# Five pairs in blocks in the mixer's three middle projections, with a pair's block sums in a tile of their own

## Chip, cores and metric

The kernel runs on one core of a Trainium2 chip. The metric is device time in microseconds, the median of several runs; a profiled execution gives the trace. The core has a matrix engine (PE; its weight loads stand on a row of their own, PEld), a vector engine (DVE), a scalar engine (ACT), GpSimd (POOL, here mostly an issuer of DMAs that add to their target) and SP (an issuer of plain DMAs).

## What is computed

One layer of a decoder trunk on x of 256 rows x 2048 columns, float32: a feed-forward half step, a mixer of two head groups (differential attention and an mLSTM) between one combined input and one output projection, a second feed-forward half step and a last norm.

```python
x = x + 0.5 * swiglu(rmsnorm(x, ffn1_norm[l]), ffn1_w_gate[l], ffn1_w_up[l], ffn1_w_down[l])
h = rmsnorm(x, mix_norm[l])
a_q, a_k, a_v, m_q, m_k, m_v, m_o, m_i, m_f = jnp.split(h @ w_in[l], split_idx, axis=-1)
...
x = x + jnp.concatenate([y_a, y_b], axis=-1) @ w_out[l]
x = x + 0.5 * swiglu(rmsnorm(x, ffn2_norm[l]), ffn2_w_gate[l], ffn2_w_up[l], ffn2_w_down[l])
return rmsnorm(x, final_norm)
```

Nearly all of the work is x (256 rows) times a weight matrix.

## The kernel before

**Products.** Weights and x are float32. Each is split in two parts of a shorter format, high and low (`split`, L130 to L133: ACT casts the high part, DVE subtracts it to get the low part), and a product is three matmuls: high x high (L181), low x high (L182) and high x low (L184), each with a stationary 128x128 piece of x and a moving 128x512 piece of the weights.

**Plain units and pairs in blocks.** Two column chunks of weights, `wa` and `wb`, of 512 columns each are worked together (`Paired`). The 2048 rows of the weights are 16 k tiles, or 8 pairs of k tiles. A pair in plain products takes, for each of the two chunks, 2 k tiles x 2 halves of x's rows: 8 products. A pair in blocks is treated as a 2x2 block matrix times a 2x2 block matrix, with seven products instead of eight (Strassen's scheme in Winograd's form): A1, A2 and B2 with pieces of x and S1, S2, S3, S4 with sums of pieces of x (`sums`, L344 to L350). The weights need sums as well, which are made in place in a `raw` tile of three pieces: two at once by DVE (L480), a second by DVE (L498) or by a DMA of POOL that adds (L496), a third by such a DMA from a later load (`late`, L534). `ns` is the number of pairs in blocks; the rest is plain. L496 is used where `ns` is over 3, for all but the last two (or the last lone) of the pairs; `twos` groups the pairs by two.

**Stages of one `Paired`.** `leading` makes A1 and S1 for each two pairs; `sums` S2, A2 (`bare`, into the accumulator `accn`) and S3; `second` B2 and S4, mixed with plain units of the first chunk; `third` is the plain units of the second chunk. `Chain.run` interleaves `third` of one `Paired` with `leading` of the next. Small work of the mixer (convolutions, gates, scores, transposes) is put in lists (`side`, `mid`, `pending`), one entry of which is taken at each step of these stages.

**x's pieces.** In `sum_pair` a pair of x gets two tiles of the pool `slots` (22 tiles of 4 KB a partition), `hi` and `lo`, of eight 128x128 pieces each: four of x itself and four sums. A pair that is only used in plain products has one tile with both (`plain_pair`). In the mixer x's pairs are made by `chunk_to_xt` while the first feed-forward part ends; the first `NP_MIX` of eight pairs have sums.

**Where blocks are used.** In the feed-forward parts `ns` is 5 for the gate and up projections. In the mixer come one q/k `Paired` of narrower chunks (392 and 384 columns, 2 pairs in blocks), and then five of two 512-column chunks of `w_in`, with `NPS_MIX` pairs in blocks; the three middle ones are at about 771 to 970 us.

**Order.** A scheduler orders each engine's instructions by priority, by the order in which the program names them and by the tiles that are free; DMAs wait in their issuer's queue in that order. `rsq` (L291 to L296) computes a power on POOL, so that it stands in POOL's queue among DMA issues.

Of the kernel before, what the change touches and what calls it, by code (L numbers as in the profile page):

```python
# [10 lines left out]
F32R = mybir.dt.float32r  # L11
# [6 lines left out]
P = 128  # L18
D = 2048
S = 256  # L20
# [11 lines left out]
NEG = -1.0e30  # L32
UK = 2
NP = 5
NP_MIX = 4
NPS_MIX = (3,4,4,4,3)
NP_QK = 2
NP_OUT = 3
NP_FIRST = 3
# [16 lines left out]
G_FFN1, G_MIX, G_FFN2, G_CW, G_CB, G_ATT, G_ML = 0, 16, 32, 48, 80, 88, 96  # L56
# [4 lines left out]
def tile_trunk_layer(ctx: ExitStack, tc: tile.TileContext, x, xt, par, bias_if, lamv, fnorm,  # L61
# [4 lines left out]
    slots = ctx.enter_context(tc.tile_pool(name="slots", bufs=22))  # L66
# [11 lines left out]
    def nm(s):  # L78
        uid[0] += 1
        return f"{s}_{uid[0]}"  # L80


    prm = const.tile([P, N_PAR], F32, name="prm")
# [41 lines left out]
    def split_gain(src, gcol, hi, lo):  # L125

        nc.scalar.activation(hi, src, AF.Copy, scale=prm[:, gcol:gcol + 1])
        nc.vector.scalar_tensor_tensor(lo, src, prm[:, gcol:gcol + 1], hi.bitcast(F32),
                                       op0=ALU.mult, op1=ALU.subtract)

    def split(src, hi, lo):
        return (nc.scalar.copy(hi, src),  # L132
                nc.vector.tensor_tensor(out=lo, in0=src, in1=hi.bitcast(F32), op=ALU.subtract))  # L133
# [11 lines left out]
    def ahead_of_splits(i, ins, slack=SLACK):  # L145
        queued[i].append((len(splits) + slack, ins))
# [38 lines left out]

    def halves(xp, k, hb):

        hi, lo = xp[k // 2]
        i = 2 * (k % 2) + hb
        return hi[:, i, :], lo[:, i, :]  # L190

    def plain_pair(xp, j):

        t = slots.tile([P, 2, UK, S], F32R, tag="s", name=nm("xt"))
        xp[j] = tuple(t[:, i, :, :].rearrange("p a (b c) -> p (a b) c", b=NT) for i in range(2))
        return t[:, 0, :, :], t[:, 1, :, :]

# [27 lines left out]
    def in_turn(load):  # L225
        for early in turns[-1:]:
            after(load, early)
        turns.append(load)
# [13 lines left out]
    def units(accs, xp, w, nk, last_units=1, ahead=None, w0=0, banks=None):  # L242
# [9 lines left out]
        def products(hbs, u, rh, rl):  # L252
            ks = [(t, u * UK + t) for t in range(UK)]
            mms([(accs[hb], *halves(xp, k, hb), rh[:, t, :], rl[:, t, :], k == 0 and not (one and hb),
                  k == nk - 1, one) for hb in hbs for t, k in ks])
# [51 lines left out]
    def chunk_to_xt(c, gbase, xp, ns, now=KD):  # L307


        def run(j):  # L310
            tr = ps_tr.tile([P, 2, S], F32, tag="tr", name=nm("tr"))
            for i in range(2):
                for hb in range(NT):
                    nc.tensor.transpose(tr[:, i, hb * P:(hb + 1) * P],  # L314
                                        xres[:, hb, (2 * j + i) * P:(2 * j + i + 1) * P], ident)
            with tc.high_priority(offset=AHEAD):
                if j < ns:
                    sum_pair(xp, j, gained(tr, prm[:, gbase + 2 * j:gbase + 2 * j + 2]), j >= now)
                else:
                    hi, lo = plain_pair(xp, j)  # L320
                    for i in range(2):
                        split_gain(tr[:, i, :], gbase + 2 * j + i, hi[:, i, :], lo[:, i, :])

        pending.extend(functools.partial(run, j) for j in (2 * c, 2 * c + 1))
# [4 lines left out]
    def gained(src, gain):  # L329
        g = wk("xg")  # L330
        for i in range(2):
            ahead_of_splits(0, act.activation(g[:, i * S:(i + 1) * S], src[:, i, :], AF.Copy, scale=gain[:, i:i + 1]))
        return g.rearrange("p (a b) -> p a b", b=P)

    def sum_tiles(xp, j):
        xp[j] = tuple(slots.tile([P, 8, P], F32R, tag="s", name=nm("xs")) for _ in range(2))
        return xp[j]

    def sum_pair(xp, j, g, put_off=False):
        hi, lo = sum_tiles(xp, j)  # L340
        split(g, hi[:, 0:4, :], lo[:, 0:4, :])
        (side.append if put_off else lambda f: f())(functools.partial(sums, g, hi, lo))

    def sums(g, hi, lo):  # L344
        s = wk("xsum").rearrange("p (a b) -> p a b", b=P)
        tt = nc.vector.tensor_tensor
        tt(out=s[:, 0:2, :], in0=g[:, 0:2, :], in1=g[:, 1:4:2, :], op=ALU.subtract)
        tt(out=s[:, 2, :], in0=s[:, 1, :], in1=g[:, 0, :], op=ALU.subtract)
        tt(out=s[:, 3, :], in0=g[:, 2, :], in1=s[:, 2, :], op=ALU.add)
        split(s, hi[:, 4:8, :], lo[:, 4:8, :])  # L350

    def add_part(acc, hb, c):

# [9 lines left out]
    def residual(accs, c, scale, parts):  # L363
        for hb in range(NT):
            add_half(accs[hb], xres[:, hb, c * CW:(c + 1) * CW], scale)
        for hb in range(NT):
            square_sum(xres[:, hb, c * CW:(c + 1) * CW], parts[:, hb, c:c + 1])
# [19 lines left out]
    def wk(name):  # L387
        return work.tile([P, CW], F32, tag="w", name=nm(name))
# [28 lines left out]
    side, mid = [], []  # L417
# [6 lines left out]
    class Paired:  # L424
# [10 lines left out]
            self.raws = []  # L435

        def job(self, acc, j, xi, w, wi, first, last, on=False):
            xh, xl = self.xp[j]
            return acc, xh[:, xi, :], xl[:, xi, :], w[0][:, wi, :], w[1][:, wi, :], first, last, on

        def load(self, j):
# [253 lines left out]


    xp1 = {}
    gs = []

    xraws = {}  # L700

    def load_xt(u, t=None):
        k, i = u * UK, u % 2 * UK
        with tc.high_priority(offset=AHEAD):
            if i == 0 and not t:
                xraws[u // 2] = slots.tile([P, 2 * UK, S], F32, tag="s", name=nm("xraw"))
            both = xraws[u // 2]
            raw = both[:, i:i + UK, :]
            if t is not None:
                in_turn(nc.sync.dma_start(raw[:, t, :], xt[:, k + t, :]))  # L710
            elif u < 2:
                in_turn(nc.sync.dma_start(raw, xt[:, k:k + UK, :]))
            elif i == 0:
                nc.sync.dma_start(both, xt[:, k:k + 2 * UK, :])
            if u < NP:
                if not t:
                    gs.append((raw, u, *sum_tiles(xp1, u)))
                hi, lo = gs[-1][2:]
                hi, lo = (t[:, 0:4, :].rearrange("p (a b) c -> p a (b c)", a=2) for t in (hi, lo))
            else:  # L720
                hi, lo = plain_pair(xp1, u)
            for j in range(UK) if t is None else (t,):
                split_gain(raw[:, j, :], G_FFN1 + k + j, hi[:, j, :], lo[:, j, :])
        if u >= KD // UK - FIRST_IN:
            sum_xt()
        if u >= KD // UK - NT:

            hb = u - (KD // UK - NT)
            with tc.high_priority(offset=AHEAD - XLATE):
                nc.sync.dma_start(xres[:, hb, :], x[hb * P:(hb + 1) * P, :])  # L730

    def sum_xt():

        raw, j, hi, lo = gs.pop(0)
        with tc.high_priority(offset=AHEAD), tc.issue_after(splits[-FIRST_SUMS][0].ins):
            sums(gained(raw, prm[:, G_FFN1 + j * UK:G_FFN1 + j * UK + UK]), hi, lo)

    r1 = {}

# [17 lines left out]
    def finish1(c, accs):  # L757
        residual(accs, c, 0.5, parts2)
        chunk_to_xt(c, G_MIX, xp2, NP_MIX, NP_QK)

    chain = Chain()
    ffn(chain, xp1, rstd1, wg1, wu1, wd1, finish1, first=(load_xt, sum_xt))


# [46 lines left out]
    def to_T(outs):  # L811

        def take(accs):
            t = mixt([P, NT, CW], name="pj")
            evac(accs, [t[:, hb, :] for hb in range(NT)])
            outs.append(col_transposes([t[:, hb, :] for hb in range(NT)], 4))

        return take
# [146 lines left out]
    def both(c, ns):  # L965
        return Paired(xp2, win[c], win[c + 1], KD, ns)
# [6 lines left out]
    qT, kT = [], []  # L973
    chain.run(both(2, NPS_MIX[0]), to_T(qT), to_T(qT))

# [40 lines left out]
    def by_head(f):  # L1016
        mid.extend(functools.partial(f, h) for h in range(NH))

    by_head(scores)
    chain.run(both(0, NPS_MIX[1]), functools.partial(take_mv, 0), functools.partial(take_mv, 1))  # L1020
    by_head(numerators)
    chain.run(both(4, NPS_MIX[2]), to_T(kT), to_T(kT))
    enm = late["enm"]
# [122 lines left out]
    by_head(attend)  # L1146
    chain.run(both(6, NPS_MIX[3]), take_av, take_av)
    chain.run(both(8, NPS_MIX[4]), functools.partial(gate_out, 0), functools.partial(gate_out, 1))

# [119 lines left out]
```

## Time and profile before

| | |
|---|---|
| median of 3 runs | 1766.78 us (1765.72 to 1767.57) |
| the profiled execution, its own time | 1765.02 us |
| its span | 1763.0 us |
| granted PE clock, mean | 0.999 |
| HBM read | 349.56 MB |

The profile is of one execution; the span goes from its first to its last instruction. Rows of groups read: line, engine, operation, output<-inputs, shapes, count | busy us, mean ns of one | idle time just before, and what ended it. `accn` is one of two accumulators that are kept over a `Paired`, `acc` any other; `wh` and `wl` are the high and low parts of weights, `xs` and `xt` x's pieces with and without sums, `raw`, `rawp` and `late` loaded weights, `xsum` sums of x before their split.

### The profile page before, as it was taken

To read this page: it belongs to the slowest core of one execution; us is meant where nothing else is said; L and a number is where in the kernel's file an instruction comes from. 1 tells how busy PE (TensorE), PEld (TensorE's weight loads), DVE (VectorE), ACT (ScalarE), POOL (GpSimd) and SP (SyncE) were. 2 spreads that over 40 slices of the span, in tenths; PEclk is the share of its full clock that TensorE was granted. 3 is DMA by queue.
4 is the path that set the end of the run, shared out by engine and by line. 5 is a ranking of instruction groups with operands and counts; after the bars stand their busy time and mean duration, and the time that the engine had idled before them with its cause. 6 is when DMAs were issued, how large, how long until landed. Compare 5 with 4: busy or idle time off the path is not lost. (4 is left out here: it accounts for less than half of the span.)

```text
span 1763.0 us, 24427 instructions
## 1 busy us (share of the span) xinstructions
PE 1750.1 (99%) x7935; PEld 1440.6 (82%) x7935; DVE 1608.9 (91%) x2174; ACT 1262.1 (72%) x1935; POOL 418.3 (24%) x615
## 2 busy tenths in 40 slices
PE   9999999999999999999999999999999999999997
PEld 7788888888888888987888888888888888888886
DVE  7989999999999999897788999999999999999997
ACT  8676676777667768776676777776777777667765
POOL 0022332322233312111121101122232332223310
PEclk9999999999999999999999999999999999999999
DMA  9797998999799977576766677997988999799973
GB/s 364 245 255 211 243 281 258 266 284 262 216 253 269 269 238 207 183 234 202 221 199 201 189 213 211 269 266 227 246 254 286 239 281 268 232 246 276 259 256 117
DMA packets 153728, 427.35 MB, mean 242 GB/s; under 512 B 17440, under 2 KB 18752, under 8 KB 153344
## 3 DMA queue, kind: packets, MB, share of 16 engines
q0 software_dynamic: 74336, 191.94, 43.4%
q1 hardware_dynamic: 78112, 231.76, 38.6%
q10 hardware_dynamic: 1152, 2.09, 0.3%
q8 instruction: 62, 1.02, 0.2%
q14 instruction: 66, 0.54, 0.1%
HBM read 349.56 MB, written 2.10 MB: 199 GB/s over the span
## 5 line engine op out<-in xcount | busy, mean ns | idle before, releaser
L132 ACT CAST wh<-raw 128x512 fp32r<-128x512 f32 (+2 forms) x870 | 584.7, 706 | 247.3 <-PE acc L182 77.0
L133 DVE TENSOR_TENSOR wl<-raw,wh 128x512 fp32r<-128x512 f32 (+2 forms) x870 | 661.5, 791 | 62.9 <-ACT wh L132 58.8
L133 DVE TENSOR_TENSOR wl<-rawp,wh 128x1024 fp32r<-128x1024 f32 (+3 forms) x314 | 370.9, 1196 | 39.8 <-ACT wh L132 35.6
L132 ACT CAST wh<-rawp 128x1024 fp32r<-128x1024 f32 (+3 forms) x314 | 320.6, 1033 | 92.7 <-PE acc L182 44.2
L181 PE MATMUL acc<-wh,xs 128*128 128x512 f32 (+2 forms) x925 | 358.5, 388 | 0.5 <-ACT us L504 0.4
L182 PE MATMUL acc<-wh,xs 128*128 128x512 f32 (+2 forms) x925 | 357.3, 387 | 0.5 <-DVE xs L133 0.5
L184 PE MATMUL acc<-wl,xs 128*128 128x512 f32 (+2 forms) x925 | 308.0, 388 | 0.2
L534 POOL DMA_DIRECT2D raw<-late x173 | 149.5, 1027 | 435.1 <-DVE wl L133 395.6
L181 PE MATMUL acc<-wh,xt 128*128 128x512 f32 (+2 forms) x592 | 228.6, 387 | 0.7 <-ACT wh L132 0.7
L182 PE MATMUL acc<-wh,xt 128*128 128x512 f32 (+2 forms) x592 | 227.5, 385 | 0.0
L181 PE MATMUL accn<-wh,xt 128*128 128x512 f32 (+1 forms) x576 | 227.0, 397 | 0.1
L182 PE MATMUL accn<-wh,xt 128*128 128x512 f32 (+1 forms) x576 | 222.9, 389 | 0.0
L480 DVE TENSOR_TENSOR raw<-raw 128x1024 f32<-128x1024 f32 x173 | 207.9, 1215 | 0.5 <-DMA raw<-in_wu_dram 0.2
L184 PEld LDWEIGHTS acc<-wl,xs 128*128 128x128 f32 x925 | 172.7, 188 | 38.0 <-DVE wl L133 3.2
L181 PEld LDWEIGHTS acc<-wh,xs 128*128 128x128 f32 x925 | 173.7, 188 | 36.2 <-ACT us L504 1.3
L182 PEld LDWEIGHTS acc<-wh,xs 128*128 128x128 f32 x925 | 173.7, 188 | 35.4 <-DVE xs L133 1.0
L184 PE MATMUL acc<-wl,xt 128*128 128x512 f32 (+2 forms) x592 | 164.2, 385 | 0.0
L184 PE MATMUL accn<-wl,xt 128*128 128x512 f32 (+1 forms) x576 | 161.7, 389 | 0.0
L181 PE MATMUL accn<-wh,xs 128*128 128x512 f32 (+1 forms) x390 | 153.6, 395 | 0.6 <-ACT wh L132 0.6
L182 PE MATMUL accn<-wh,xs 128*128 128x512 f32 (+1 forms) x390 | 152.0, 391 | 0.0
L496 POOL DMA_DIRECT2D raw<-raw x86 | 73.4, 871 | 310.0 <-DVE wl L133 281.8
L184 PE MATMUL accn<-wl,xs 128*128 128x512 f32 (+1 forms) x390 | 135.8, 390 | 0.2 <-DVE wl L133 0.2
(229 smaller groups left out, 2133.7 us busy)
## 6 DMA issues: line engine op xcount, KB each, us to landing
rawp<-in_wd_dram SPq DMA_DIRECT2D x88, 512.0 KB, 5.6
raw<-late POOLq DMA_DIRECT2D x171, 256.0 KB, 5.1
raw<-in_wu_dram POOLq DMA_DIRECT2D x80, 512.0 KB, 7.7
rawp<-in_wu_dram SPq DMA_DIRECT2D x73, 512.0 KB, 5.0
rawp<-in_wg_dram SPq DMA_DIRECT2D x69, 512.0 KB, 5.2
raw<-in_wd_dram POOLq DMA_DIRECT2D x44, 512.0 KB, 7.5
rawp<-in_win_dram SPq DMA_DIRECT2D x44, 512.0 KB, 5.0
raw<-raw POOLq DMA_DIRECT2D x86, 256.0 KB, 4.2
```

Source lines behind the costliest of these rows:

```text
L132: return (nc.scalar.copy(hi, src), nc.vector.tensor_tensor(out=lo, in0=src, in1=hi.bitcast(F32), op=ALU.subtract))
L133: nc.vector.tensor_tensor(out=lo, in0=src, in1=hi.bitcast(F32), op=ALU.subtract))
L181: nc.tensor.matmul(acc, lh, rh, start=first, stop=False, skip_group_check=on)
L182: nc.tensor.matmul(acc, ll, rh, start=False, stop=False, skip_group_check=on)
L184: newest[:] = [nc.tensor.matmul(acc, lh, rl, start=False, stop=last, skip_group_check=on)]
L480: nc.vector.tensor_tensor(out=raw[:, 0:2, :], in0=raw[:, 0:3:2, :], in1=raw[:, 1:2, :].to_broadcast([P, 2, n]), op=ALU.add)
L496: nc.gpsimd.dma_start(raw[:, 0, :], raw[:, 2, :], accum_op=ALU.add)
L534: nc.gpsimd.dma_start(self.raws[j][:, 0, :], lates[-1][1][:, i, :], accum_op=ALU.add)
```

## The change

A pair's four pieces of x are now in a tile like that of a plain pair (high and low together), and its four sums in a second tile, taken only when the sums are made. So the second tile is free again after the pair's last block product, while the first stays for the plain products. The bytes are the same. `NP_MIX` is 5 and `NPS_MIX` (3, 5, 5, 5, 3): in the three middle projections of the mixer one pair more is in blocks, and one pair more of the mixer's x has sums.

```diff
-NP_MIX = 4
-NPS_MIX = (3,4,4,4,3)
+NP_MIX = 5
+NPS_MIX = (3, 5, 5, 5, 3)
...
-        hi, lo = xp[k // 2]
+        hi, lo = xp[k // 2][:2]
...
-    def plain_pair(xp, j):
+    def plain_pair(xp, j, name="xt"):
...
-        t = slots.tile([P, 2, UK, S], F32R, tag="s", name=nm("xt"))
+        t = slots.tile([P, 2, UK, S], F32R, tag="s", name=nm(name))
...
-    def sum_tiles(xp, j):
-        xp[j] = tuple(slots.tile([P, 8, P], F32R, tag="s", name=nm("xs")) for _ in range(2))
-        return xp[j]
-
     def sum_pair(xp, j, g, put_off=False):
-        hi, lo = sum_tiles(xp, j)
-        split(g, hi[:, 0:4, :], lo[:, 0:4, :])
-        (side.append if put_off else lambda f: f())(functools.partial(sums, g, hi, lo))
+        plain_pair(xp, j, "xs")
+        split(g, *xp[j])
+        (side.append if put_off else lambda f: f())(functools.partial(sums, g, xp, j))
 
-    def sums(g, hi, lo):
+    def sums(g, xp, j):
...
-        split(s, hi[:, 4:8, :], lo[:, 4:8, :])
+        t = slots.tile([P, 2, 4, P], F32R, tag="s", name=nm("xs"))
+        xp[j] += t[:, 0, :, :], t[:, 1, :, :]
+        split(s, *xp[j][2:])
...
         def job(self, acc, j, xi, w, wi, first, last, on=False):
-            xh, xl = self.xp[j]
+            xh, xl = self.xp[j][2 * (xi // 4):][:2]
+            xi %= 4
```

The first feed-forward part's loading of x (`load_xt`, `sum_xt`) is changed in the same way. Lines move up by one to four: L347 becomes L343, L496 becomes L495, L534 becomes L533.

How the order of instructions moves, at two places. The first is DVE at the end of the first feed-forward part, at about 693 to 697 us, before the change; `wl` from `late` is the low part of the q/k projection's late weights, the numbers tell tiles apart.

```order
L128 SCALAR_TENSOR_TENSOR xt_6511<-tr_6506,prm,xt_6511 128x256
L361 SCALAR_TENSOR_TENSOR xres<-acc_6121,xres 128x512
L347 TENSOR_TENSOR xsum_6367<-xg_6348 128x256
L347 TENSOR_TENSOR xsum_6401<-xg_6360 128x256
L348 TENSOR_TENSOR xsum_6367<-xsum_6367,xg_6348 128x128
L133 TENSOR_TENSOR wl_6600<-late_6580,wh_6599 128x784
L349 TENSOR_TENSOR xsum_6367<-xg_6348,xsum_6367 128x128
L348 TENSOR_TENSOR xsum_6401<-xsum_6401,xg_6360 128x128
```

The same place after the change, from the second sum operation on:

```order
L344 TENSOR_TENSOR xsum_6365<-xsum_6365,xg_6348 128x128
L359 SCALAR_TENSOR_TENSOR xres<-acc_6121,xres 128x512
L345 TENSOR_TENSOR xsum_6365<-xg_6348,xsum_6365 128x128
L343 TENSOR_TENSOR xsum_6400<-xg_6359 128x256
L344 TENSOR_TENSOR xsum_6400<-xsum_6400,xg_6359 128x128
L345 TENSOR_TENSOR xsum_6400<-xg_6359,xsum_6400 128x128
L343 TENSOR_TENSOR xsum_6517<-xg_6511 128x256
L344 TENSOR_TENSOR xsum_6517<-xsum_6517,xg_6511 128x128
L345 TENSOR_TENSOR xsum_6517<-xg_6511,xsum_6517 128x128
L133 TENSOR_TENSOR wl_6608<-late_6588,wh_6607 128x784
```

All sum operations of three pairs (nine) now stand ahead of the split of the late weights; before, three of the six of two pairs did.

The second place is POOL's queue in the third of the middle projections, before the change: the last loads of the next projection's first pair, the second sums (L496), the power that `rmh` is (L295), and late additions (L534).

```order
L447 DMA raw_8819<-in_win_dram 128x512
L208 DMA raw_8819<-in_win_dram 128x1024
L496 DMA raw_8324<-raw_8324 128x512
L496 DMA raw_8327<-raw_8327 128x512
L295 TENSOR_TENSOR rmh_8278<-rsqv_8276,mhalf 128x8
L534 DMA raw_8324<-late_8466 128x512
L534 DMA raw_8327<-late_8466 128x512
```

The same place after the change:

```order
L446 DMA raw_8468<-in_win_dram 128x512
L208 DMA raw_8468<-in_win_dram 128x1024
L495 DMA raw_8366<-raw_8366 128x512
L495 DMA raw_8369<-raw_8369 128x512
L495 DMA raw_8416<-raw_8416 128x512
L495 DMA raw_8419<-raw_8419 128x512
L295 TENSOR_TENSOR rmh_8338<-rsqv_8336,mhalf 128x8
L533 DMA raw_8366<-late_8527 128x512
```

There are four second sums ahead of `rmh` and not two, and the load ahead of them is that of this projection's own fifth pair (`raw` has five tiles), where it was the next projection's first.

More of the change, by code (lines that the diff above doesn't have):

```diff
@@ L697, in tile_trunk_layer @@
     xp1 = {}
-    gs = []
+    gs, halves1 = [], []
     xraws = {}
@@ L714, in load_xt @@
                 nc.sync.dma_start(both, xt[:, k:k + 2 * UK, :])
[L715 to L721, printed above, removed]
+            if not t:
+                if u < NP:
+                    gs.append((raw, u))
+                halves1[:] = plain_pair(xp1, u, "xs" if u < NP else "xt")
+            hi, lo = halves1
             for j in range(UK) if t is None else (t,):
@@ L732, in sum_xt @@
     def sum_xt():
-        raw, j, hi, lo = gs.pop(0)
+        raw, j = gs.pop(0)
         with tc.high_priority(offset=AHEAD), tc.issue_after(splits[-FIRST_SUMS][0].ins):
-            sums(gained(raw, prm[:, G_FFN1 + j * UK:G_FFN1 + j * UK + UK]), hi, lo)
+            sums(gained(raw, prm[:, G_FFN1 + j * UK:G_FFN1 + j * UK + UK]), xp1, j)
     r1 = {}
```

## The prediction

> **What bounds the kernel now.** I read the page's busy times first, then the busy time by stage, then the spacing of matmuls inside the stage that is changed, then the waits there.
>
> ```profile
> span 1763.0 us, 24427 instructions
> PE 1750.1 (99%) x7935; PEld 1440.6 (82%) x7935; DVE 1608.9 (91%) x2174; ACT 1262.1 (72%) x1935; POOL 418.3 (24%) x615
> ```
>
> PE is busy for all but 13 us of the span. A busy PE need not be a PE at its pace, so the stages and the spacing have to be seen. The next view is the busy time by stretch: 200 to 600 us and 1200 to 1600 us are the two feed-forward parts, which already run five pairs in blocks; 771 to 970 us holds the three middle projections; the others are places that the steps below need.
>
> ```profile
> 200.00:600.00 400.00, 400.00 (x1785) 329.36 (x1784) 375.41 (x471) 287.14 (x419) 122.36 (x177) 1.00 0.91 258
> 650.00:700.00 50.00, 49.44 (x230) 40.45 (x228) 49.81 (x76) 39.66 (x75) 8.26 (x12) 1.00 0.67 195
> 690.00:710.00 20.00, 20.00 (x110) 18.29 (x108) 19.52 (x36) 16.39 (x32) 4.50 (x7) 1.00 0.78 222
> 780.00:790.00 10.00, 10.00 (x46) 8.02 (x45) 10.00 (x20) 8.44 (x13) 2.60 (x3) 1.00 0.60 139
> 771.00:970.00 199.00, 199.00 (x924) 162.25 (x923) 162.44 (x257) 141.62 (x253) 38.47 (x59) 1.00 0.69 204
> 926.00:950.00 24.00, 24.00 (x113) 19.63 (x112) 21.89 (x33) 15.81 (x23) 3.76 (x5) 1.00 0.66 181
> ```
>
> After each stretch's length come the busy times of PE, PEld, DVE, ACT and POOL, then the granted clock. In the middle projections PE is busy for 199.00 of 199 us at full clock, DVE for 162.44 (82%), ACT for 141.62 (71%). The timeline of PE, inside the second of them, gives the pace:
>
> ```profile
> 862.61 0.39 PE L182 MATMUL accn<-wh,xt 128*128 128x512 f32 x1
> 862.83 1.07 PE L184 MATMUL accn<-wl,xt 128*128 128x512 f32 x4
> 863.74 0.39 PE L181 MATMUL accn<-wh,xs 128*128 128x512 f32 x1
> ```
>
> From 862.61 to 863.74 five matmuls of 128x512 start: 1.13 / 5 = 0.226 us each. So a matmul that is left out here is worth 0.226 us, as long as nothing else becomes late. The waits of PE's weight loads from 771 to 970 us (total, times, longest) say how much else is late today:
>
> ```profile
> PEld L983 <- issue: 1.3, 4, 0.3
> PEld rr L982 <- issue: 1.2, 4, 0.4
> PEld accn L181 <- ACT accn L504: 0.7, 4, 0.2
> ```
>
> No weight split is among the larger ones. PE bounds this stage, and DVE, its nearest follower, has 37 us to spare in 199.
>
> **Part 1: fewer matmuls.** A pair in plain products costs 2 column chunks x 2 k tiles x 2 row halves = 8 products, in blocks 7 (A1, S1, S2, A2, S3, B2, S4); each product is three matmuls. One pair more in each of three projections takes away 3 x 1 x 3 = 9 matmuls of 128x512: 9 x 0.226 = **-2.03 us**, on the engine that bounds.
>
> By the Trainium skill (TensorE: Matmul & The Clock Gate, section "Back-to-back issue gap") a stream of weight load and matmul pairs should keep about 131 ns a matmul at 512 columns, which would make the term -1.18 us and the forecast 1766.1 (an estimate). This trace disagrees: 226 ns, and the trace decides.
>
> **Part 2: more work on ACT and DVE.** The groups by line and shape give the prices (busy time, mean ns):
>
> ```profile
> L133 DVE TENSOR_TENSOR wl<-raw,wh 128x512 fp32r<-128x512 f32 x686 | 448.3, 684 | 43.9 <-ACT wh L132 40.7 <-PE acc L184 1.7 <-PE accn L184 0.6
> L132 ACT CAST wh<-raw 128x512 fp32r<-128x512 f32 x686 | 402.8, 620 | 209.9 <-PE acc L182 58.6 <-DVE raw L480 57.9 <-DMA raw<-in_wg_dram 35.1
> L133 DVE TENSOR_TENSOR wl<-rawp,wh 128x1024 fp32r<-128x1024 f32 x294 | 354.0, 1219 | 35.4 <-ACT wh L132 32.8
> L132 ACT CAST wh<-rawp 128x1024 fp32r<-128x1024 f32 x294 | 305.5, 1052 | 83.4 <-PE acc L182 38.0 <-PE accn L182 38.0 <-issue 4.0
> L480 DVE TENSOR_TENSOR raw<-raw 128x1024 f32<-128x1024 f32 x171 | 205.9, 1218 | 0.5 <-DMA raw<-in_wu_dram 0.2
> L498 DVE TENSOR_TENSOR raw<-raw 128x512 f32<-128x512 f32 x85 | 56.5, 686 | 0.8
> L347 DVE TENSOR_TENSOR xsum<-xg 128x256 f32<-128x256 f32 x17 | 7.0, 418 | 2.9 <-ACT xg L412 2.9
> L348 DVE TENSOR_TENSOR xsum<-xsum,xg 128x128 f32<-128x128 f32 x17 | 4.9, 286 | 0.2
> L349 DVE TENSOR_TENSOR xsum<-xg,xsum 128x128 f32<-128x128 f32 x17 | 4.9, 286 | 0.1
> L133 DVE TENSOR_TENSOR xs<-xsum,xs 128x512 fp32r<-128x512 f32 x39 | 26.5, 684 | 1.4 <-ACT xs L132 1.4
> L128 DVE SCALAR_TENSOR_TENSOR xt<-tr,prm,xt 128x256 fp32r<-128x256 f32 x14 | 6.3, 478 | 0.0
> ```
>
> Per projection the fifth pair brings five splits of 128x512 (A1, S1, S2, A2, S3) and one of 128x1024 (B2 with S4), and takes away two of 128x1024. On DVE that is 5 x 0.684 - 1.219 = 2.20 us, and the first weight sum is 1.218 more; of the second sums, two were on DVE (pairs 2 and 3) and one will be (pair 4), -0.686. Together 2.73 us, **8.20 us** for three. On ACT it is 5 x 0.620 - 1.052 = 2.05, 6.1 us for three. DVE in 771 to 970 us comes to 162.4 + 8.2 = 170.6 of some 197 us, 87%. The feed-forward rows show five pairs with DVE at 375.41 of 400 (94%) and PE at 400.00 of 400. That cover hides the whole of it: I take **0** for the mean load.
>
> The cover is thinner locally. While the weights of the first of the three are prepared, DVE is busy 10.00 of 10 (780 to 790 us), and the fifth pair's A1, S1 and first sum need 2 x 0.684 + 1.218 = 2.59 us of DVE beside six matmuls, 6 x 0.226 = 1.36: 1.23 us more than PE takes. Also one step of the list of side work, a convolution, is taken one call earlier, since leading now has three calls and not two. From 926 to 950 us one plain unit moves out of the stretch (12 matmuls, 2.71 us of PE; 1.22 us of DVE): DVE 21.89 of 24 becomes 20.67 of 21.29, 97%. If that cover fails, it costs 1.23 us each time; rival A has that.
>
> **Part 3: one pair more of the mixer's x has block sums** (five for four), made while the feed-forward part ends. DVE: three sum operations 0.418 + 0.286 + 0.286, splits of the pair and of its sums 2 x 0.684, less two plain splits 2 x 0.478: **+1.40 us**, at 690 to 710 us, where it is busy 19.52 of 20 already. 19.52 + 1.40 is 0.92 over. The nine sum operations now stand in one run ahead of the split of the late weights; in that place were two plain splits and three sum operations, so that split comes 3 x 0.990 - (2 x 0.478 + 2 x 0.418 + 0.286) = 0.89 us later. What it has to spare is in these two rows, of DVE and of PE (start, duration):
>
> ```profile
> 695.89 0.97 DVE L133 TENSOR_TENSOR wl<-late,wh 128x784 fp32r<-128x784 f32 x1
> 699.77 0.52 PE L184 MATMUL accn<-wl,xs 128*128 128x392 f32 x2
> ```
>
> Written by 696.86, used at 699.77: 2.9 us ahead. So the cost lies between 0 and 0.92. The nearest row is 650 to 700 us, where DVE at 49.81 of 50 left PE without work for 0.56; I take **+0.5 us**. A gain here is excluded: nothing is removed from an engine that PE waits for.
>
> **Part 4: POOL.** It issues five pair loads and not four in each, four second sums by DMA and not two, and five late additions. Behind the second sums, in the third projection, stands rmh, for which DVE waits in its turn:
>
> ```profile
> 885.51 0.17 DVE L412 TENSOR_TENSOR fm<-rmh,dd 128x8 f32<-128x8 f32 x1 [1.79 <-POOL rmh L295]
> L496 POOL DMA_DIRECT2D raw<-raw x32: 832/848/872, 193.5 to 590.4; - x32
>   ACT wh L132: 3.4, 7
> DMA to landing us min/median/max: 3.3/4.2/7.8
> ```
>
> (The last three are of the second sums by DMA from 100 to 600 us.) Two more issues of 0.85 us are 1.7, while DVE does a split and a sum, 0.684 + 0.686 = 1.37: the wait of 1.79 grows by some 0.3, and everything queued on DVE behind fm with it. PE does not feel the 1.79 today; I take 0, with 0.3 as the upper end. The landing of pairs 2 and 3 is rival B.
>
> **Part 5: the sums in a tile of their own.** The same number of bytes is written and read by the same instructions; the high halves wait for ACT and the low halves for DVE as before, so 0. It changes when tiles are taken, and so the order of the first splits. The wait of PE that could go or double by that is this one:
>
> ```profile
> 53.30 0.50 PE L181 MATMUL acc<-wh,xt 128*128 128x512 f32 x1 [0.72 <-ACT wh L132]
> ```
>
> I take 0, between -0.72 and +0.72.
>
> **Sum.** The profiled execution took 1765.02 us (span 1763.0 and 2.0 around it): 1765.02 - 2.03 + 0.5 = 1763.5. It lies 1.76 below the median of the runs, 1766.78 (1765.72 to 1767.57). On the scale of that median the forecast is 1766.78 - 1.53 = **1765.2 us**, -0.09%. A change under 0.2% (3.5 us) is about what a measurement of this kernel can't tell from none.
>
> **The rivals.**
>
> A, slower: DVE becomes the bound where block products are prepared. The mechanism is the 1.23 us by which the fifth pair asks more of DVE than of PE. It decides from the point where DVE's lead over PE (2.9 us in the rows above) is used up. Three times 1.23, the 0.92 of part 3, the 0.3 of part 4 and one convolution, three operations that I price with the 478 ns row (1.4), make 6.3; less 2.03 it is +4.3: 1771.1. For it speak the 10.00 of 10; against it, the feed-forward parts with 94% on DVE and no lost PE time.
>
> B, slower: the second sums of pairs 2 and 3, given from DVE to DMA, land late. By DVE they took 2 x 0.686 = 1.37; by DMA the second comes 0.85 + 4.2 after the split, 3.7 later. PE's cover is the lone fifth pair's A1 and S1 (1.36), a last plain unit (2.71) and the first two pairs' S2 (1.36), 5.4. It decides when landing takes over 5.9; at 7.8, the longest seen, it costs 1.9 a projection: +5.7 - 2.03, 1770.4. Against it: 32 such sums in 500 us made ACT wait 3.4 us in all and PE not at all. The Trainium skill (SBUF — State Buffer, section "Who interferes with whom") has a rule that speaks for it: GpSimd can't write descriptors while DVE holds the shared ports. Here the issues last 832 to 872 ns, beside a DVE that is busy 94%, so no such blocking shows.
>
> C, nothing gained: PE's free 2.03 us come back as waits of that size for DVE, which trades bound with PE: 1766.8. The 97% from 926 to 950 us speaks for it.
>
> D, more than forecast: part 3 costs nothing, the 0.72 of part 5 and the 0.56 lost from 650 to 700 us go as well: 1766.78 - 2.03 - 0.72 - 0.56 = 1763.5. Both waits come from the order of short operations, which is new at those places.
>
> **How the numbers follow.** Forecast 0.61, C 0.14, D 0.16, A 0.06, B 0.03. D lies at the edge of 0.2%, so half of it counts as faster: 0.08. A and B lie beyond it on the other side, 0.08 with a little left to the middle. The range reaches from D, with a little of the runs' scatter, to past C with the same scatter, 1763.1 to 1768.0, and leaves out A, B and the ends of D.
>
> **What would show it.** Right: PE's spacing stays 0.226 us, 9 matmuls of 128x512 fewer, DVE busy some 9.6 us more in all, and the stretch from the first middle projection's evacuation to the last one's half about 2 us shorter with PE at 100%. Wrong: new waits of PE for wl or wh between 771 and 960 us of over 1 us together (A), ACT waiting for DMA raw<-raw there with PE idle behind it (B), or a stretch that is no shorter with PE idle (C).

## The result and the profile after

| | before | after |
|---|---|---|
| median | 1766.12 us (22 runs, 1764.13 to 1772.47) | 1763.67 us (22 runs, 1761.57 to 1767.95) |
| profiled execution, own time | 1765.02 us | 1762.31 us |
| its span | 1763.0 us | 1760.5 us |

The ratio is 0.9984, 95% interval 0.9978 to 0.9990: 2.45 us by the medians. The interval lies wholly under 1, and the ratio is within the 0.2% that the text on record took as the least that can be told from no change. With 22 runs on each side it can be told, just. Two runs of the study, one of the kernel before (7480.27 us) and one with four pairs at both ends (1940.04 us, at a clock of 0.85), were slow and enter no ratio.

The first lines of the page after:

```profile
span 1760.5 us, 24489 instructions
PE 1747.8 (99%) x7926; PEld 1438.5 (82%) x7926; DVE 1616.8 (92%) x2189; ACT 1267.6 (72%) x1949; POOL 430.5 (24%) x630
```

PE has 7926 matmuls and not 7935, nine fewer; DVE is busy 7.9 us more, ACT 5.5, POOL 12.2, each against its row before. The busy times by stretch (PE, PEld, DVE, ACT, POOL, then the granted clock), for the stretches shown of before:

```profile
650.00:700.00 50.00, 49.44 (x229) 40.53 (x229) 49.30 (x77) 39.11 (x74) 8.28 (x12) 1.00 0.68 199
690.00:710.00 20.00, 20.00 (x111) 18.57 (x110) 19.32 (x36) 16.65 (x33) 4.51 (x7) 1.00 0.78 218
780.00:790.00 10.00, 10.00 (x46) 8.02 (x45) 9.96 (x19) 7.64 (x12) 1.71 (x2) 1.00 0.80 172
771.00:970.00 199.00, 199.00 (x925) 162.18 (x924) 171.17 (x271) 148.60 (x268) 49.55 (x74) 1.00 0.75 216
926.00:950.00 24.00, 24.00 (x113) 19.61 (x112) 22.44 (x37) 17.28 (x32) 4.83 (x8) 1.00 0.65 176
```

From 771 to 970 us DVE went from 162.44 to 171.17 us and ACT from 141.62 to 148.60, and PE still has 199.00 of 199. All of the extra work lies beside the matmuls. The largest waits of PE's weight loads there are the same as before, to the tenth (total, times, longest):

```profile
PEld L980 <- issue: 1.3, 4, 0.3
PEld rr L979 <- issue: 1.2, 4, 0.4
PEld accn L181 <- ACT accn L503: 0.7, 4, 0.2
```

**Where the time came from.** A span says nothing of the place, and the time at which the mixer starts varies: over the profiles of this study, PE's wait for `us` came between 670.65 and 673.22 us. So the stretch is measured between two waits of PE that most of these kernels have, the one for `us` ahead of the mixer and the one for `xs` behind the three middle projections. The timeline of PE before:

```profile
671.08 0.50 PE L181 MATMUL acc<-wh,xs 128*128 128x512 f32 x1 [0.45 <-ACT us L504]
980.53 0.50 PE L182 MATMUL acc<-wh,xs 128*128 128x512 f32 x1 [0.53 <-DVE xs L133]
```

and after, with the wait at the start of the kernel that could have gone or doubled:

```profile
53.04 0.50 PE L181 MATMUL acc<-wh,xt 128*128 128x512 f32 x1 [0.72 <-ACT wh L132]
671.00 0.50 PE L181 MATMUL acc<-wh,xs 128*128 128x512 f32 x1 [0.45 <-ACT us L503]
978.17 0.50 PE L182 MATMUL acc<-wh,xs 128*128 128x512 f32 x1 [0.54 <-DVE xs L133]
```

The stretch is 980.53 - 671.08 = 309.45 us before and 978.17 - 671.00 = 307.17 after, 2.28 shorter. The three waits themselves are the same within 0.01 us (0.72, 0.45, 0.53 before). The spacing of matmuls, on PE's timeline inside the second projection, did not change either:

```profile
863.60 0.39 PE L182 MATMUL accn<-wh,xs 128*128 128x512 f32 x1
863.83 0.39 PE L181 MATMUL acc<-wh,xs 128*128 128x512 f32 x1
...
864.51 0.39 PE L184 MATMUL acc<-wl,xs 128*128 128x512 f32 x1
```

From 863.60 to 864.51 four matmuls start, 0.91 / 4 = 0.227 us each.

### The profile page after: what moved, and what is told of

Same layout as the page of the kernel before. It is cut to its first block, busy times and chain, and to the rows that moved or that the text cites. A ratio compares the mean times of both kernels' runs of the same rounds, so it can differ in the third digit from the quotient of the medians.

```text
span 1760.5 us, 24489 instructions
## 1 busy us (share of the span) xinstructions
PE 1747.8 (99%) x7926; PEld 1438.5 (82%) x7926; DVE 1616.8 (92%) x2189; ACT 1267.6 (72%) x1949; POOL 430.5 (24%) x630
## 5 line engine op out<-in xcount | busy, mean ns | idle before, releaser
L132 ACT CAST wh<-raw 128x512 fp32r<-128x512 f32 (+2 forms) x885 | 596.1, 707 | 250.3 <-PE acc L182 79.9
L133 DVE TENSOR_TENSOR wl<-raw,wh 128x512 fp32r<-128x512 f32 (+2 forms) x885 | 673.5, 792 | 61.1 <-ACT wh L132 55.7
L133 DVE TENSOR_TENSOR wl<-rawp,wh 128x1024 fp32r<-128x1024 f32 (+3 forms) x308 | 363.7, 1196 | 34.3 <-ACT wh L132 29.3
L181 PE MATMUL acc<-wh,xs 128*128 128x512 f32 (+2 forms) x956 | 370.0, 388 | 0.5 <-ACT us L503 0.5
L182 PE MATMUL acc<-wh,xs 128*128 128x512 f32 (+2 forms) x956 | 368.6, 386 | 0.5 <-DVE xs L133 0.5
L184 PE MATMUL acc<-wl,xs 128*128 128x512 f32 (+2 forms) x956 | 317.6, 387 | 0.2
L533 POOL DMA_DIRECT2D raw<-late x176 | 152.5, 1046 | 424.0 <-DVE wl L133 362.0
L181 PE MATMUL acc<-wh,xt 128*128 128x512 f32 (+2 forms) x564 | 218.3, 388 | 0.7 <-ACT wh L132 0.7
L181 PE MATMUL accn<-wh,xt 128*128 128x512 f32 (+1 forms) x552 | 217.5, 396 | 0.1
L182 PE MATMUL acc<-wh,xt 128*128 128x512 f32 (+2 forms) x564 | 217.3, 386 | 0.0
L182 PE MATMUL accn<-wh,xt 128*128 128x512 f32 (+1 forms) x552 | 213.8, 390 | 0.0
L181 PEld LDWEIGHTS acc<-wh,xs 128*128 128x128 f32 x956 | 179.5, 188 | 36.8 <-ACT us L503 1.1
L182 PEld LDWEIGHTS acc<-wh,xs 128*128 128x128 f32 x956 | 179.6, 188 | 36.2 <-DVE xs L133 1.0
L181 PE MATMUL accn<-wh,xs 128*128 128x512 f32 (+1 forms) x408 | 160.7, 395 | 0.5 <-ACT wh L132 0.5
L182 PE MATMUL accn<-wh,xs 128*128 128x512 f32 (+1 forms) x408 | 158.9, 391 | 0.0
L184 PE MATMUL acc<-wl,xt 128*128 128x512 f32 (+2 forms) x564 | 157.3, 386 | 0.0
L495 POOL DMA_DIRECT2D raw<-raw x92 | 78.7, 880 | 309.7 <-DVE wl L133 246.5
```

The costliest lines, as they stand in the source:

```text
L132: return (nc.scalar.copy(hi, src), nc.vector.tensor_tensor(out=lo, in0=src, in1=hi.bitcast(F32), op=ALU.subtract))
L181: nc.tensor.matmul(acc, lh, rh, start=first, stop=False, skip_group_check=on)
L182: nc.tensor.matmul(acc, ll, rh, start=False, stop=False, skip_group_check=on)
L184: newest[:] = [nc.tensor.matmul(acc, lh, rl, start=False, stop=last, skip_group_check=on)]
L495: nc.gpsimd.dma_start(raw[:, 0, :], raw[:, 2, :], accum_op=ALU.add)
L533: nc.gpsimd.dma_start(self.raws[j][:, 0, :], lates[-1][1][:, i, :], accum_op=ALU.add)
```

## The experiments

The theory: nine matmuls of 0.226 us go, and what DVE, ACT and POOL do more is hidden by the lead that they have over PE. The rivals on record: DVE becomes the bound (A), the adding transfers land late (B), nothing is gained (C), other waits go too (D). In the table the stretch is that between the two waits above; ratios are to the kernel before, with the 95% interval. The kernel before was run again beside each group of runs, with medians of 1766.59, 1766.35 and 1767.03 us, and a row's ratio is to the runs beside it, so medians of different rows compare only to about 1 us.

| kernel | stretch, us | median, us | ratio |
|---|---|---|---|
| before | 309.45 | 1766.12 | 1 |
| after | 307.17 | 1763.67 | 0.9984 [0.9978, 0.9990] |
| tile alone | 309.23 | 1764.85 | 0.9992 [0.9983, 1.0002] |
| sums made, not used | 309.11 | 1765.03 | 0.9991 [0.9983, 1.0000] |
| five pairs, old tiles | 307.24 | 1764.19 | 0.9987 [0.9978, 0.9995] |
| two pairs in the middle | 313.29 | 1770.44 | 1.0025 [1.0015, 1.0035] |
| 15 DVE operations more | 308.21 | 1765.12 | 0.9994 [0.9985, 1.0002] |
| 30 DVE operations more | 312.48 | 1768.94 | 1.0017 [1.0008, 1.0026] |
| second sums on DVE | 307.21 | 1762.32 | 0.9976 [0.9967, 0.9986] |
| four pairs in the first | 310.80 | 1764.67 | 0.9987 [0.9974, 0.9999] |
| four pairs in the last | - | 1772.38 | 1.0041 [1.0025, 1.0057] |
| four at both ends | - | 1773.63 | 1.0042 [1.0029, 1.0055] |
| four at both, sums on DVE | - | 1772.22 | 1.0040 [1.0024, 1.0056] |
| five in all five | - | 1781.34 | 1.0086 [1.0073, 1.0099] |

(Where a dash stands, the second wait is another one, so the stretch can't be read.)

### The parts of the change one by one

The new tile alone, the changed kernel with the old numbers:

```diff
-NP_MIX = 5
-NPS_MIX = (3, 5, 5, 5, 3)
+NP_MIX = 4
+NPS_MIX = (3, 4, 4, 4, 3)
```

> The sums in a tile of their own, with the old numbers (four pairs with sums in the mixer, 3, 4, 4, 4, 3 in blocks). If the whole gain is the matmuls left out, the time is that of before: span 1763.0 within 0.3 us, ratio 1.000. If the new order of the first splits, which the new tile brings, is worth the 0.4 us by which the changed kernel is already ahead at 771 us, the span is about 1762.6 and the lead is there at 771 us. If the tile that is given back earlier were the source of the gain, the span would be about 1760.5.

The fifth pair's sums of x made, but not used by any product:

```diff
-NPS_MIX = (3, 5, 5, 5, 3)
+NPS_MIX = (3, 4, 4, 4, 3)
```

> As the changed kernel, but the three middle projections keep four pairs in blocks; the fifth pair's block sums are made and never used. It prices the sums alone. Forecast's step: +0.5 us (0 to 0.92) against the tile alone, lost by PE between 690 and 720 us. Rival: 0, since the weights' split has 2.9 us to spare. Either way no gain: span 1762.6 to 1763.5.

The new numbers in the kernel before, with its old tiles:

```diff
-NP_MIX = 4
-NPS_MIX = (3,4,4,4,3)
+NP_MIX = 5
+NPS_MIX = (3,5,5,5,3)
```

> The kernel before with the new numbers alone (five pairs with sums, 3, 5, 5, 5, 3 in blocks), sums and pieces still in the same two tiles. If the count of matmuls is all, it is as fast as the changed kernel: 2.0 us under before, span 1761.0 within 0.4. If the tiles of the pool run short, since each of five pairs now keeps two tiles to the end of the mixer's projections, PE waits in the last projection or the output projection, and the span is longer by a wait of 1 us or more.

The stretches fall in two groups. With four pairs it is 309.45, 309.23 and 309.11 us (mean 309.26), with five pairs 307.17 and 307.24 (mean 307.21). The difference, 2.06 us, is the nine matmuls (2.03), and neither the tile nor the sums belong to it: from the tile alone to the sums made and not used, the stretch changes by -0.12 us. The sums did add work to DVE at the place where they were priced. The same row of the sums-unused kernel and of the tile-alone kernel:

```profile
690.00:710.00 20.00, 20.00 (x111) 18.51 (x111) 19.32 (x36) 16.27 (x32) 4.50 (x7) 1.00 0.76 218
```

```profile
690.00:710.00 20.00, 20.00 (x111) 18.38 (x110) 18.54 (x35) 15.52 (x30) 4.50 (x7) 1.00 0.77 216
```

DVE has 0.78 us more in these 20 (19.32 for 18.54), and PE is at 20.00 in both. The kernel with the old tiles gains as much as the changed one, so the new tile is not what makes the gain possible. Its span, 1759.5 us, lay under the 1761.0 within 0.4 that was expected by the count.

The whole times alone would not show this. The intervals of these four kernels overlap, and the tile alone and the unused sums have ratios of 0.9992 and 0.9991, some 1.4 to 1.6 us under the kernel before, of which the stretch shows 0.2 to 0.3. Whether the rest is scatter or a gain outside the stretch is open; the case for the matmuls rests on the stretch.

### The price of a pair

Two pairs instead of five in the three middle projections, 27 matmuls more:

```diff
-NPS_MIX = (3, 5, 5, 5, 3)
+NPS_MIX = (3, 2, 2, 2, 3)
```

> The changed kernel with two pairs in blocks in each of the three middle projections (3, 2, 2, 2, 3): nine pairs fewer than the changed kernel, six fewer than before. If a pair is worth its three matmuls and nothing else, PE needs 9 x 3 x 0.226 = 6.1 us more than in the changed kernel: span 1766.6, and between PE's waits at 670 and 977 us 307.1 + 6.1 = 313.2. If DVE shares the bound (rival C), the loss is well under that, since DVE has some 24 us less to do: between 0 and 4 us.

PE's timeline of that kernel:

```profile
671.90 0.50 PE L181 MATMUL acc<-wh,xs 128*128 128x512 f32 x1 [0.45 <-ACT us L503]
985.19 0.50 PE L182 MATMUL acc<-wh,xs 128*128 128x512 f32 x1 [0.52 <-DVE xs L133]
```

313.29 us, as expected by the count (313.2), and 6.12 more than after: 6.12 / 27 = 0.2267 each. From two to five pairs the gain is in proportion to the matmuls, though DVE's work in 771 to 968 us goes from 140.54 to 169.17; the rows with two pairs and after:

```profile
771.00:968.00 197.00, 197.00 (x916) 160.48 (x915) 140.54 (x219) 130.24 (x227) 21.11 (x34) 1.00 0.58 187
```

```profile
771.00:968.00 197.00, 197.00 (x916) 160.53 (x915) 169.17 (x269) 146.60 (x265) 49.55 (x74) 1.00 0.76 218
```

So nothing of the fifth pair is eaten by a new wait. The start times of the matmuls say the same. Add up, over 771 to 968 us, what each distance from one start to the next has above 0.227 us: it is 4.87 us with two pairs, 4.86 before (four) and 4.94 after (five). Call this sum the excess; most of it is there in every kernel, where matmuls of other shapes stand between.

### How much lead DVE has: rival A

Work that does nothing, put on DVE behind the first weight sum of each pair in the three middle projections; once (15 operations of 0.68 us) and twice (30). It does not change the values:

```diff
+for _ in range(getattr(self, "fills", 0)):
+    nc.vector.tensor_tensor(out=raw[:, 1, :], in0=raw[:, 1, :], in1=raw[:, 1, :], op=ALU.max)
...
-return Paired(xp2, win[c], win[c + 1], KD, ns)
+p = Paired(xp2, win[c], win[c + 1], KD, ns)
+p.fills = 1 if ns == 5 else 0
+return p
```

> The changed kernel with one DVE operation more (128x512, two inputs, 0.684 us, a maximum of a weight piece with itself, which leaves it as it is) behind the first weight sum of each of the 15 pairs in blocks of the three middle projections: 10.3 us more of DVE, 169 to 179.5 of 197 us, 91%. If DVE's lead covers, as it did for the fifth pair's 8.2 us, the span stays at 1760.5 within 0.4. If the cover was just used up by the fifth pair, all of it shows: up to 1770.8.

> The same with two such operations a pair: 20.5 us more of DVE, 190 of 197, 96%, all of it where A1 and S1 are prepared. There the five pairs ask DVE for 5 x (2.59 + 1.37) = 19.8 us and four plain units for 4.9, 24.7 in all, while PE has 6.8 + 10.9 = 17.7 us of work: 7 us over, more than the lead of 2.9. Expected by rival A's mechanism: some 2 to 4 us lost in each, span 1766 to 1773. If the mean load decided, nothing would be lost.

The stretch grows by 1.04 us with 15 operations and by 5.31 with 30. (By their durations they are 10.2 and 20.2 us, about what the expectations say. The page's busy time of DVE grew by only 7.0 and 15.5: all other DVE operations were together 2 to 3 us shorter in these executions, under 0.2%, and 0.4 and 2.5 us more of the operations overlapped.) With 15, neither expectation was met, neither no cost nor all of it. The busy times by stretch with 15:

```profile
771.00:968.00 197.00, 196.81 (x910) 159.32 (x909) 175.66 (x283) 145.74 (x264) 49.93 (x74) 1.00 0.76 217
```

and with 30, with the waits of PE's weight loads from 735 to 1015 us:

```profile
771.00:968.00 197.00, 194.56 (x891) 155.09 (x890) 181.10 (x291) 141.03 (x257) 48.55 (x73) 1.00 0.74 217
```

```profile
PEld acc L184 <- DVE wl L133: 3.3, 6, 1.0
PEld acc L181 <- ACT wh L132: 3.2, 5, 1.1
```

These are rival A's waits, and here they are made on purpose. At a DVE of 175.66 of 197 us (89%) PE begins to lose, at 181.10 (92%) it loses 2.44 us of busy time and more in spacing. The changed kernel, at 169.17 (86%), is below that point, but not far: the mechanism of A exists, and begins within 6.5 us more of busy time, if the work comes at this place.

The three projections are not alike. With 15 operations the excess is 6.02 us, 1.08 over after, and the loss lies in the first projection alone: 2.50 us from 771 to 820 us (1.47 after), and 3.52 in the rest (3.38 after). All waits of PE's weight loads for `wh` or `wl` come between 782.57 and 803.02 us. The same five operations cost next to nothing in the second and the third. With 30 the excess is 10.07 us, and some 1.3, 1.4 and 2.4 us are lost in the three, where 2 to 4 were expected in each.

### Late transfers: rival B

All second sums of the middle projections by DVE instead of by DMA:

```diff
-return Paired(xp2, win[c], win[c + 1], KD, ns)
+return Paired(xp2, win[c], win[c + 1], KD, ns, by_dma=ns != 5)
```

> The changed kernel, but all second sums of the three middle projections are made by DVE (four each were given to DMAs that add, twelve in all): 12 x 0.686 = 8.2 us more DVE work there, and no transfer to wait for. Theory (DVE's lead decides, and the transfers land in time): the stretch from the wait for us at 671 us to the one for xs at 980 us, 307.2 us in the changed kernel, grows by 0.3 to 1.0, as with the 10.3 us of filler (1.0). Rival B (the transfers land late): it gets shorter, by up to 2 us.

```profile
771.00:968.00 197.00, 197.00 (x916) 160.54 (x915) 175.16 (x281) 146.59 (x265) 39.27 (x62) 1.00 0.67 202
```

The stretch is 307.21, 0.04 from the changed kernel's: both expectations missed. A gain from the transfers and a loss from DVE could cancel in this number, but both kernels have the same excess, 4.94 us, within 0.1 us of that with two and four pairs, so there is no loss to cancel. And in the changed kernel nothing waits for the twelve transfers from 771 to 970 us. Their time from issue to landing:

```profile
DMA to landing us min/median/max: 3.3/3.9/6.5
```

So the transfers cost nothing. And 6.0 us more DVE (175.16) costs nothing either, at nearly the same busy time at which the filler cost 1.04 us. So the mean load alone does not decide. The two runs differ in place and in amount (15 operations and 12): the filler stands behind the first sums of the weights, the second sums come later, when DVE is likely further ahead. Which of the two counts was not separated. The median, 1762.32, is the lowest of the study, but its interval overlaps that of the changed kernel, and the stretch is the same, so it isn't shown to be faster.

### More pairs at the ends

The same step in the first and the last of the five projections; four pairs at both, then each alone, then five in all:

```diff
-NPS_MIX = (3, 5, 5, 5, 3)
+NPS_MIX = (4, 5, 5, 5, 4)
```

> The changed kernel with four pairs in blocks in the first and last 512-column projections, where all five lost 8 and 11 us (4, 5, 5, 5, 4). Two pairs, 6 matmuls fewer: -1.36 us, span 1759.1, if DVE's cover holds for one pair. If DVE is already at its end there, PE waits for wl between 740 and 800 us or between 975 and 1010 us, and the span is over 1760.5.

> The changed kernel with four pairs in blocks, not three, in the first of the five projections only: 3 matmuls fewer, -0.7 us by count. The kernel with four in the first and the last was 10 us slower than the changed kernel. Theory, from its trace: the first projection's part of that is the excess of PE's spacing from 750 to 800 us, some 2.6, so this one is 2 to 3 us slower than the changed kernel. Rival (the last projection alone carries the loss): it is 0.7 us faster.

> The changed kernel with four pairs in blocks, not three, in the last of the five projections only: -0.7 us by count. Theory, from the trace with four at both: PE's spacing there lost some 7 us between 950 and 1050 us, so this one is 6 to 8 us slower than the changed kernel. Rival (the losses of the two ends need each other, through the raw tiles): under 3 us slower.

> The changed kernel with five pairs in blocks in the first and last of the mixer's 512-column projections as well (5, 5, 5, 5, 5). Four pairs more, 12 matmuls fewer: 12 x 0.226 = 2.7 us, span 1757.8 if DVE's cover holds. Rival A of the prediction: the first stands where DVE is over 99% busy (650 to 700 us) with convolutions and gates beside it, and the last beside the transposes of the mixer's output; there the cover fails, PE waits for wl, and the span is 1760.5 or longer.

By the medians the first projection costs 1.0 us (2 to 3 were expected), the last 8.7 (6 to 8 expected), both 10.0, and five everywhere 17.7. The 1.0 is within the scatter; the stretch of the profiled execution is 3.63 longer, of which some 1.4 is a fall of the clock (last section). The losses of the two ends add up within the scatter, and most of it is in the last one. There PE's weight loads wait for both splits; with four pairs in the last, from 935 to 1015 us:

```profile
PEld acc L181 <- ACT wh L132: 5.0, 7, 2.3
PEld acc L184 <- DVE wl L133: 3.1, 4, 1.4
```

In the changed kernel no wait for `wh` or `wl` is among the seven largest from 735 to 1015 us. In the first projection the loss begins with one wait. The timeline of ACT with four pairs in the first (start, duration):

```profile
749.47 0.62 ACT L132 CAST wh<-raw 128x512 fp32r<-128x512 f32 x1 [2.52 <-DMA raw<-raw]
...
751.30 1.05 ACT L132 CAST wh<-late 128x1024 fp32r<-128x1024 f32 x1
...
752.97 0.62 ACT L132 CAST wh<-raw 128x512 fp32r<-128x512 f32 x1
```

and of PE:

```profile
751.47 0.40 PE L182 MATMUL acc<-wh,xs 128*128 128x512 f32 x1
753.65 0.50 PE L181 MATMUL acc<-wh,xs 128*128 128x512 f32 x1 [1.78 <-ACT wh L132]
```

ACT stood 2.52 us for the transfer that adds the second sum; the cast that PE needed was behind that in ACT's queue and began at 752.97. That is rival B's mechanism, in a place where there is not yet a lead. To test whether the transfers explain the ends:

```diff
-NPS_MIX = (3, 5, 5, 5, 3)
+NPS_MIX = (4, 5, 5, 5, 4)
...
-return Paired(xp2, win[c], win[c + 1], KD, ns)
+return Paired(xp2, win[c], win[c + 1], KD, ns, by_dma=ns != 4)
```

> Four pairs in blocks at both ends (1773.6 us), but the second sums of these two projections by DVE, not by DMA: two each, four in all, 4 x 0.686 = 2.7 us more DVE work, four issues of 0.85 us fewer in POOL's queue. Theory that DVE's load makes the ends slow: another 1 to 3 us slower, 1775 to 1777. Rival, POOL's queue and its transfers make them slow: faster than 1773.6 by 2 us or more.

1772.22 against 1773.63 us: 1.4 us faster, between the two expectations, and the intervals overlap. The wait at 751 us is gone; in its place matmuls that wait for `wl` start 0.67 us late at 763.82 and 1.05 late at 767.28. One engine's lateness is exchanged for another's. What exactly makes the last projection late (ACT and DVE also do the attention's last steps there) stays open.

## Why the prediction was right, point by point

The forecast was 1765.2 us in a range of 1763.1 to 1768.0, with 0.84 on a difference within 0.2%; measured, 1763.67 us and, by the ratio, -0.16%. The mechanism held and one term was mis-sized.

- **Part 1, nine matmuls, -2.03.** Measured 2.06 as the mean over five profiles, 0.2267 us each with 27. The price by the Trainium skill (TensorE: Matmul & The Clock Gate, section "Back-to-back issue gap"), 131 ns, would have made it 1.18; the smallest difference between a kernel with four pairs and one with five is 309.11 - 307.24 = 1.87.
- **Part 2, DVE and ACT hidden.** DVE was forecast at 170.6 of some 197 us and measured at 169.17 in 771 to 968 us, with no new wait. In all DVE is busy 7.9 us more, where 9.6 were forecast: the durations grew by 10.9, but 3.0 of it overlap. The two thin places held: from 780 to 790 us DVE is busy 9.96 of 10 (10.00 before), from 926 to 950 us 22.44 of 24, 94% (91% before) where 97% was worked out, and PE is at 10.00 and 24.00.
- **Part 3, the sums of x, +0.5: the mis-sized step.** It measured about 0 (-0.12 between two kernels that differ in nothing else). The step took the nearest row, 0.56 us lost from 650 to 700 us, as a sign that more DVE work would lengthen that wait. Most of it is the wait for `us`, 0.45 before and after, which ends on ACT ahead of the place where the sums stand; so it was the wrong neighbour. The right one was quoted beside it: the late weights' split is 2.9 us ahead of its matmul. After, DVE's and PE's rows are:

```profile
697.27 0.97 DVE L133 TENSOR_TENSOR wl<-late,wh 128x784 fp32r<-128x784 f32 x1
```

```profile
699.65 0.52 PE L184 MATMUL accn<-wl,xs 128*128 128x392 f32 x2
```

  Written by 698.24, used at 699.65: 1.41 us ahead. The split moved back by 1.38 us, 1.50 against PE's matmul, where 0.89 was forecast, and the cover of 2.9 took it.
- **Part 4, POOL.** The wait for `rmh` did not grow by 0.3; it is 1.79 again:

```profile
885.86 0.17 DVE L410 TENSOR_TENSOR fm<-rmh,dd 128x8 f32<-128x8 f32 x1 [1.79 <-POOL rmh L295]
```

- **Part 5, the tile, 0.** In the stretch -0.22 us with four pairs (309.23 for 309.45), and -0.07 with five (307.17 for 307.24). The wait at 53 us is 0.72 in both.
- **The rivals.** A and B did not decide, but both mechanisms could be made: A with 15 operations more on DVE, B in the first projection. The longest landing in the middle projections, 6.5 us, is over B's limit of 5.9, and nothing waited; whether it was one of the pairs that B counts was not read. C fell, since the stretch is shorter. The time came out at D's 1763.5, but not by D: its first part (the sums cost nothing) held, but the waits of 0.72 and 0.45 that it would have removed are still there. That the number is D's is chance.
- **The rest.** From 1765.2 to 1763.67 are 1.53 us: 0.66 is the kernel before, whose median over 22 runs is 1766.12 and not 1766.78; 0.5 is part 3; 0.37 is left, small beside the 2.57 us by which the start of the mixer varies over the profiles. So 0.66 of the miss is the three runs from which the forecast started, and no step of the argument.

## What to carry to other kernels

Price an edit on the bounding engine by instructions times their spacing, and check it with a multiple of the edit (27 matmuls tell the price better than nine). Whether the work it adds elsewhere is hidden is not read from the mean load: 6.0 us more of DVE's busy time cost nothing in one place, 6.5 in another cost 1.04, and that all in one of three projections. So read, place by place, how long before its use each result is written. Where spans vary by as much as the effect, measure between two waits that both kernels have.

## What the runs showed of the hardware

A short wait of PE can cost more than itself, when the granted clock falls after it. With four pairs in the first projection, the busy times around the wait at 751.47 us (the clock is the third figure from the right):

```profile
750.00:755.00 5.00, 3.22 (x15) 2.33 (x15) 3.98 (x6) 5.00 (x11) 2.87 (x6) 1.00 1.00 213
755.00:760.00 5.00, 5.00 (x17) 3.93 (x16) 4.42 (x7) 4.71 (x9) 0.46 (x1) 0.66 0.90 213
```

The matmul behind the wait came 1.95 us late, and from 1.6 us later on, 755.27 to 758.26, seven matmuls were 0.427 us apart (756.98, 757.40, 757.83 among them) in place of 0.226: 7 x 0.2 = 1.4 us on top. With four at both ends and the sums on DVE the same followed on a delay of 2.44 us at 979 us (clock 0.66 from 980 to 985 us). It does not always come: with four at both ends, delays of 1.84 us at 751 and 2.07 at 981 left the clock at 1.00, and so did one of 2.04 at 979 with four in the last. The Trainium skill (TensorE: Matmul & The Clock Gate, section "Why this matters for your kernels") puts the limit at idle gaps of over about 3 us; here 1.95 and 2.44 were enough in two of five cases.

The clock's own records say more than these five. With four in the first, the ends on DVE and five in all five, the clock is 0.50 for 3.41 us each time (from 754.97, 981.39 and 995.83 us), and each fall comes 220, 286 and 289 times 3.413 us after the clock first became full (at 4.03, 5.18 and 9.37 us). So the falls lie on a grid of steps. The busy times of the step before the fall and of the fall, with four in the first:

```profile
751.56:754.97 3.41, 1.63 (x8) 1.11 (x7) 2.65 (x5) 3.41 (x7) 1.68 (x5) 1.00 1.06 184
754.97:758.38 3.41, 3.41 (x10) 2.64 (x9) 2.83 (x5) 3.12 (x7) 0.49 (x1) 0.50 0.93 170
```

and at the same place with four at both ends, where the clock stayed:

```profile
750.74:754.15 3.41, 1.73 (x8) 1.14 (x7) 2.65 (x5) 3.41 (x7) 1.67 (x5) 1.00 1.02 193
754.15:757.56 3.41, 3.41 (x16) 2.79 (x16) 3.23 (x6) 3.41 (x7) 0.85 (x1) 1.00 0.96 153
```

PE was idle for 1.78 us of the step before that fall, and for 2.05 and 2.21 before the other two; where the clock stayed, for 1.68 and 1.40 (the delay of 2.07 lies across two steps) and 1.69. So what seems to count is how much of a wait falls into one step, and that shifts from one execution to the next. It is a reading of six cases, not a shown rule: at the end of two kernels (after, and the tile alone) a step with 1.92 and 1.91 us idle was followed by a full clock.

DVE's operations overlap where they follow each other without a wait. The timeline of DVE with 15 operations more (start, duration):

```profile
787.73 0.67 DVE L133 TENSOR_TENSOR wl<-raw,wh 128x512 fp32r<-128x512 f32 x1
788.33 0.67 DVE L482 TENSOR_TENSOR raw<-raw 128x512 f32<-128x512 f32 x1
788.93 0.67 DVE L133 TENSOR_TENSOR wl<-raw,wh 128x512 fp32r<-128x512 f32 x1
```

They start 0.60 us apart and last 0.67 each. So in a full queue an operation of 128x512 takes 0.60 us of DVE's time, and a price from the mean duration of a group, 0.684, is 14% too high. The sums of part 2 and of the fillers, made with durations, are upper ends in this sense.
